# Chunks of 32 rows in place of 16, with descriptors up to 64 KB, in a streaming RMSNorm + ReLU

## Chip, cores, metric

One NeuronCore of one Trainium2 chip. The metric is the device time of one execution in microseconds (us).

## The reference

```python
# x: (16, 1024, 512) float32, gamma: (512,) float32, eps: 1e-5
def reference(x, gamma, eps):
    rms = np.sqrt(np.mean(x ** 2, axis=-1, keepdims=True) + eps)
    return np.maximum(x / rms * gamma, 0).astype(np.float32)
```

That is 16,384 rows of 2 KB: 33.55 MB in, 33.55 MB out, and little arithmetic. Each of the 128 partitions gets 128 rows.

## The kernel before

Rows come in chunks of 16 per partition into six slots of a ring in SBUF, are normalised in place and are stored from there. One queue, that of SyncE (SP), issues all the large transfers in a fixed order. ScalarE (ACT) takes the sums of squares and the square root, VectorE (DVE) the rest, in groups of 8 rows.

```python
K = 16; G = 8; nslots = 6; per = K // G        # 8 chunks, 16 groups
xv = x2.rearrange("(c p k) d -> c p k d", p=P, k=K)   # 16 rows of a partition: 32 KB in one run
loads = [(0, 0, G), (0, G, K - G)] + [(i, 0, K) for i in range(1, nchunks)]

def store(i):
    nc.sync.wait_ge(done, per * (i + 1))
    nc.sync.dma_start(out=ov[i], in_=slot_ap(i)).then_inc(sem_slot[i % nslots], 16)

# ... SyncE's order:
for m, (i, a, r) in enumerate(loads):
    if i < nslots:
        load(m)                        # seven loads fill the ring
nc.sync.wait_ge(tick3, 6)              # hold: third row of VectorE's group 6
store(0); store(1)
for s in range(2):
    nc.sync.wait_ge(sem_slot[s], 32)   # store s has landed
    load(7 + s)                        # the last two chunks
nc.sync.wait_ge(tick1, 11)             # hold: first row of group 11
for i in range(2, nchunks):
    store(i)
# ... VectorE, for each group of 8 rows:
#   reciprocal (8 columns), then 8 x scalar_tensor_tensor (row * rstd * gamma),
#   with tick1 and tick3 counted at rows 0 and 2, then tensor_scalar_max over 8 rows -> done += 1
# ... SyncE at the end: waits for all stores
```

## Time and profile before

| | before |
|---|---|
| time, median of the first 3 runs | 162.25 us (162.23 to 162.32) |
| span of the profiled run | 160.4 us |
| packets of the transfer queue, share of 16 engines | 97.6% |
| VectorE busy | 126.0 us, 79% |
| VectorE's last instruction ends | 146.5 us |
| last packet ends | 158.8 us |

How to read this: when one resource is busy for 97.6% of the span, the others matter only where they make it wait. So the useful views are those of the stretches in which it could wait: the start, the end, and every place where a store waits for VectorE or a load for a store. The lines are in the prediction.

In addition to the views I read the packets' own records in the trace (size, start, duration). The records don't name the engine; I take a chain of packets that follow each other without a break to be one of the 16 DMA engines.

### The profile page before, as it was taken

Reading aid. Unit: us, or ns where it says so; the run is one execution under the profiler, and the core shown is the slowest. Engines: PE = TensorE matmul, PEld = TensorE weight load, DVE = VectorE, ACT = ScalarE, POOL = GpSimd, SP = SyncE. Lnnn points to the kernel's source line nnn. Section 1 sums busy time; section 2 is a strip of 40 time slices with the busy share of each in tenths; the row PEclk is TensorE's granted clock in tenths of the full one; section 3 lists DMA queues with packets and bytes.
Section 4 is the critical chain, followed back from the end, with each engine's and each line's share of the span. In section 5 each row is a group of like instructions: output and inputs, shape, how many; then the busy total and the mean of one; then the engine's idle time right before and its main releaser. Section 6 shows DMA issues by size and latency. Waiting matters only on the chain. (4 is left out here: it accounts for less than half of the span.)

```text
span 160.4 us, 1008 instructions
## 1 busy us (share of the span) xinstructions
DVE 126.0 (79%) x164; ACT 86.3 (54%) x273; POOL 0.2 (0%) x4
## 2 busy tenths in 40 slices
DVE  1103989898989999999999999999999999995000
ACT  3088919889989988988910298899400000000000
POOL 0000000000000000000000000000000000000000
DMA  5999999999999999999999999999999999999993
GB/s 168 419 441 437 490 400 400 499 409 392 482 433 392 433 474 400 409 499 400 392 466 433 409 425 466 417 400 482 425 392 482 425 400 474 433 400 466 425 409 139
DMA packets 2456, 67.12 MB, mean 419 GB/s; under 512 B 276, under 2 KB 276, under 8 KB 280
## 3 DMA queue, kind: packets, MB, share of 16 engines
q1 hardware_dynamic: 2448, 67.11, 97.6%
q10 hardware_dynamic: 8, 0.01, 0.0%
HBM read 33.56 MB, written 33.55 MB: 419 GB/s over the span
## 5 line engine op out<-in xcount | busy, mean ns | idle before, releaser
L152 DVE SCALAR_TENSOR_TENSOR slots<-slots,rstd,gamma_sb 128x512 f32 x128 | 86.2, 747 | 4.8 <-DVEq L149 4.8
L128 ACT ACTIVATE junk<-slots 128x512 f32 x128 | 74.5, 582 | 22.2 <-ACTq L124 22.0
L163 DVE TENSOR_SCALAR slots<-slots x16 | 36.7, 2294 | 2.4 <-DVEq L162 0.2
L128 ACT ACTIVATION_READ_ACCUMULATOR junk<-slots x128 | 23.9, 187 | 0.0
L146 DVE RECIPROCAL rstd<-rms x16 | 3.2, 197 | 6.2 <-DVEq L142 6.2
L135 ACT ACTIVATE rms<-ss,eps_sb x16 | 4.8, 301 | 3.0 <-ACTq L134 3.0
L139 DVE LOAD_MASK_SELECT gamma_sb<-gseed x1 | 0.0, 14 | 6.0 <-DMA gseed<-in_gamma_dram 6.0
L120 ACT ACT_TABLE_LOAD x1 | 1.3, 1283 | 2.8 <-issue 2.8
L113 DVE MEMSET gseed<- 128x512 f32 x1 | 0.5, 485 | 1.1 <-SPq L93 1.1
L139 DVE STREAM_SHUFFLE gamma_sb<-gseed 128x512 f32<-128x512 f32 x1 | 0.7, 716 | 0.0
L188 POOL MEMSET const-bfloat16-1.0<- 128x1 bf16 x1 | 0.1, 102 | 0.0
L188 POOL MEMSET const-uint8-127<- 128x1 uint8 x1 | 0.1, 102 | 0.0
L188 POOL MEMSET const-float32-1.0<- 128x1 f32 x1 | 0.1, 99 | 0.0
L188 POOL MEMSET const-float32-0.0<- 128x1 f32 x1 | 0.1, 98 | 0.2 <-issue 0.2
L114 DVE MEMSET eps_sb<- 128x1 f32 x1 | 0.1, 59 | 0.0
## 6 DMA issues: line engine op xcount, KB each, us to landing
out_dram<-slots SPq DMA_DIRECT2D x8, 4096.0 KB, 20.7
slots<-in_x_dram SPq DMA_DIRECT2D x7, 4096.0 KB, 30.3
slots<-in_x_dram SPq DMA_DIRECT2D x2, 2048.0 KB, 9.6
gseed<-in_gamma_dram ACTq DMA_DIRECT2D x1, 8.0 KB
```

The lines of the kernel that those rows point to most:

```text
L113: nc.vector.memset(gseed, 0.0).then_inc(sem_z, 1)
L114: nc.vector.memset(eps_sb, eps).then_inc(sem_z, 1)
L120: nc.scalar.preload_act_table(ACTF.Sqrt)
L128: a = nc.scalar.activation(out=junk[:, j, :], in_=slots[:, bass.ds(base + j * d, d)], func=ACTF.Square, accum_out=ss[:, bass.ds(col + j, 1)])
L135: nc.scalar.activation(out=rms[:, bass.ds(col, G)], in_=ss[:, bass.ds(col, G)], func=ACTF.Sqrt, bias=eps_sb, scale=inv_d).then_inc(sq, 1)
L139: nc.vector.stream_shuffle(gamma_sb, gseed, [0] * 32)
L146: nc.vector.reciprocal(out=rstd[:, bass.ds(col, G)], in_=rms[:, bass.ds(col, G)]).then_inc(sv, 1)
L152: r = nc.vector.scalar_tensor_tensor(out=row, in0=row, scalar=rstd[:, bass.ds(col + j, 1)], in1=gamma_sb, op0=ALU.mult, op1=ALU.mult)
L163: nc.vector.tensor_scalar_max(out=blk, in0=blk, scalar1=0.0).then_inc(done, 1)
L188: nc = _bacc.Bacc("TRN2", target_bir_lowering=False, num_devices=1)
```

## The change

Fewer and larger transfers: chunks of 32 rows (64 KB in one run per partition), a ring of three chunks, first and last chunk in pieces so that the pipeline starts and ends early, and stores held back until the loads' last packets are near.

```diff
-    K = 16
-    nslots = 6
+    K = 32
+    room = 3 * K
...
-    loads = [(0, 0, G), (0, G, K - G)] + [(i, 0, K) for i in range(1, nchunks)]
+    order = [(L, 0, 0, 8), (L, 0, 8, 8), (L, 0, 16, 16), (L, 1, 0, 32), (L, 2, 0, 32),
+             (S, 0, 0, 8), (S, 0, 8, 24),
+             (L, 3, 0, 8), (L, 3, 8, 24),
+             (S, 1, 0, 32), (S, 2, 0, 32), (S, 3, 0, 16), (S, 3, 16, 16)]
+    sems = [tc.alloc_semaphore(f"t{m}") for m in range(len(order))]
...
-        nc.sync.wait_ge(tick3, 6)
-        store(0)
-        store(1)
-        for s in range(2):
-            nc.sync.wait_ge(sem_slot[s], 32)
-            load(7 + s)
-        nc.sync.wait_ge(tick1, 11)
-        for i in range(2, nchunks):
-            store(i)
+        for m, (kind, i, a, r) in enumerate(order):
+            if (kind, i, a) == (S, 0, 0):
+                nc.sync.wait_ge(tick, 6)          # second row of group 6
+            elif (kind, i, a) == (S, 1, 0):
+                nc.sync.wait_ge(done, 10)
+            elif kind == L and i == 3:
+                stored(0, a, r)
+            transfer(m)                           # a store waits for its groups in `done`
...
-                if j == 0:
-                    r.then_inc(tick1, 1)
-                if j == 2:
-                    r.then_inc(tick3, 1)
+                if j == 1:
+                    r.then_inc(tick, 1)
```

An entry (L or S, chunk, first row, rows) is a load or a store.

More of the change, by code (lines that the diff above doesn't have):

```diff
@@ L32 @@
     inv_d = 1.0 / d
-    K = 16
     G = 8
+    ngroups = rows // G
+    K = 32
     nchunks = rows // K
-    nslots = 6
-    ngroups = rows // G
-    per = K // G
+    room = 3 * K
     xv = x2.rearrange("(c p k) d -> c p k d", p=P, k=K)
@@ L51 @@
     rstd = singles.tile([P, rows], F32, name="rstd")
-    slots = singles.tile([P, nslots * K * d], F32, name="slots")
+    buf = singles.tile([P, room * d], F32, name="buf")
     junk = psum.tile([P, G, d], F32, name="junk")
-    loads = [(0, 0, G), (0, G, K - G)] + [(i, 0, K) for i in range(1, nchunks)]
-    sem_half = tc.alloc_semaphore("half")
-    sem_slot = [tc.alloc_semaphore(f"slot{s}") for s in range(nslots)]
+    L, S = 0, 1
+    order = [(L, 0, 0, 8), (L, 0, 8, 8), (L, 0, 16, 16), (L, 1, 0, 32), (L, 2, 0, 32),
[3 more added lines that the diff above has]
+    sems = [tc.alloc_semaphore(f"t{m}") for m in range(len(order))]
     sem_g = tc.alloc_semaphore("gam")
@@ L64 @@
     sq = tc.alloc_semaphore("sq")
-    tick1 = tc.alloc_semaphore("tick1")
-    tick3 = tc.alloc_semaphore("tick3")
+    tick = tc.alloc_semaphore("tick")
     done = tc.alloc_semaphore("done")
@@ L69 @@
     sv = tc.alloc_semaphore("sv")
-    def slot_ap(i):
-        s = (i % nslots) * K * d
-        return slots[:, s:s + K * d].rearrange("p (k d) -> p k d", d=d)
-    def load(m):
-        i, a, r = loads[m]
-        nc.sync.dma_start(out=slot_ap(i)[:, a:a + r, :],
-                          in_=xv[i][:, a:a + r, :]
-                          ).then_inc(sem_half if m == 0 else sem_slot[i % nslots], 16)
-    def loaded(engine, m):
-        i = loads[m][0]
-        if m == 0:
-            engine.wait_ge(sem_half, 16)
-        else:
-            engine.wait_ge(sem_slot[i % nslots], 32 * (i // nslots) + 16)
@@ L88, in store, with transfer @@
-    def store(i):
-        nc.sync.wait_ge(done, per * (i + 1))
-        nc.sync.dma_start(out=ov[i], in_=slot_ap(i)).then_inc(sem_slot[i % nslots], 16)
+    def transfer(m):
+        kind, i, a, r = order[m]
+        row = (i * K) % room + a
+        here = buf[:, row * d:(row + r) * d].rearrange("p (k d) -> p k d", d=d)
+        there = (ov if kind == S else xv)[i][:, a:a + r, :]
+        if kind == S:
+            nc.sync.wait_ge(done, (i * K + a + r) // G)
+            nc.sync.dma_start(out=there, in_=here).then_inc(sems[m], 16)
+        else:
+            nc.sync.dma_start(out=here, in_=there).then_inc(sems[m], 16)
@@ L92, with stored @@
+    def stored(i, a, r):
+        nc.sync.wait_ge(sems[order.index((S, i, a, r))], 16)
     ctx.enter_context(tc.manual_schedule(engines={mybir.EngineType.SP}))
     with tc.tile_critical():
-        for m, (i, a, r) in enumerate(loads):
-            if i < nslots:
-                load(m)
-        nc.sync.wait_ge(tick3, 6)
-        store(0)
-        store(1)
-        for s in range(2):
-            nc.sync.wait_ge(sem_slot[s], 32)
-            load(7 + s)
-        nc.sync.wait_ge(tick1, 11)
-        for i in range(2, nchunks):
-            store(i)
@@ L109 @@
-        for m, (i, a, r) in enumerate(loads):
-            loaded(nc.gpsimd, m)
-            nc.gpsimd.sem_inc(ready, r // G)
+        for m, (kind, i, a, r) in enumerate(order):
[6 more added lines that the diff above has]
+            transfer(m)
+        for m, (kind, i, a, r) in enumerate(order):
+            if kind == L:
+                nc.gpsimd.wait_ge(sems[m], 16)
+                nc.gpsimd.sem_inc(ready, r // G)
@@ L124 @@
             nc.scalar.sem_inc(ready, -1)
-            base = nc.scalar.snap((gi % (nslots * per)) * (G * d))
+            base = nc.scalar.snap((gi % (room // G)) * (G * d))
             col = nc.scalar.snap(gi * G)
@@ L128 @@
                 a = nc.scalar.activation(
-                    out=junk[:, j, :], in_=slots[:, bass.ds(base + j * d, d)],
+                    out=junk[:, j, :], in_=buf[:, bass.ds(base + j * d, d)],
                     func=ACTF.Square, accum_out=ss[:, bass.ds(col + j, 1)])
@@ L142 @@
             nc.vector.sem_inc(sq, -1)
-            base = nc.vector.snap((gi % (nslots * per)) * (G * d))
+            base = nc.vector.snap((gi % (room // G)) * (G * d))
             col = nc.vector.snap(gi * G)
-            blk = slots[:, bass.ds(base, G * d)]
+            blk = buf[:, bass.ds(base, G * d)]
             nc.vector.reciprocal(out=rstd[:, bass.ds(col, G)],
@@ L150 @@
             for j in range(G):
-                row = slots[:, bass.ds(base + j * d, d)]
+                row = buf[:, bass.ds(base + j * d, d)]
                 r = nc.vector.scalar_tensor_tensor(
@@ L165 @@
     with nc.sync.register("landed") as landed:
-        nc.sync.reg_mov(landed, 32)
-        for s in range(nchunks - nslots, nslots):
-            nc.sync.wait_ge(sem_slot[s], landed)
-        nc.sync.reg_mov(landed, 64)
-        for s in range(nchunks - nslots):
-            nc.sync.wait_ge(sem_slot[s], landed)
+        nc.sync.reg_mov(landed, 16)
+        for m, (kind, i, a, r) in enumerate(order):
+            if kind == S:
+                nc.sync.wait_ge(sems[m], landed)
 _INS = ['x', 'gamma', 'eps']
```

## The prediction

> **What bounds the kernel now.** I read the page's busy shares first, then the 40 slices, then the DMA queues, then the timeline of the queue that issues the transfers. From the page:
>
> ```profile
> span 160.4 us, 1008 instructions
> ...
> DVE 126.0 (79%) x164; ACT 86.3 (54%) x273; POOL 0.2 (0%) x4
> ...
> DVE  1103989898989999999999999999999999995000
> ACT  3088919889989988988910298899400000000000
> ...
> DMA  5999999999999999999999999999999999999993
> ...
> q1 hardware_dynamic: 2448, 67.11, 97.6%
> ```
>
> The DMA row is full from the second slice to the last but one, and the queue line puts its packets at 97.6% of sixteen engines' span: 0.976 x 160.4 = 156.5 us per DMA engine. Only 3.9 us are not packet time. VectorE (DVE) ends four slices earlier. The stretches view says the same:
>
> ```profile
> 0.00:4.00 4.00, 0.49 (x2) 1.24 (x1) 0.20 (x4) 1.00 0.55 168
> 4.00:56.00 52.00, 39.90 (x53) 40.99 (x133) 0.00 (x0) 1.00 1.00 433
> ...
> 76.00:84.00 8.00, 7.55 (x11) 4.70 (x16) 0.00 (x0) 1.00 0.93 393
> ```
>
> The last two columns are DMA share and GB/s; packets are booked where they start, so short stretches wobble. The kernel is bound by the DMA engines, and a change can win only by (a) cheaper packets, (b) fewer gaps, (c) a shorter head or tail. But one chain runs close beside them:
>
> ```profile
> 0.94 3.62 SPq L77 DMA_DIRECT2D slots<-in_x_dram  x7
> 58.35 0.82 SPq L90 DMA_DIRECT2D out_dram<-slots  x2
> 71.54 10.28 SPq L77 DMA_DIRECT2D slots<-in_x_dram  x2
> 98.23 48.62 SPq L90 DMA_DIRECT2D out_dram<-slots  x6
> ```
>
> The last store is issued near 146.5 us (98.23 + 48.62 is its end), when VectorE's last group is done (next lines). It sits right behind the seventh store.
>
> ```profile
> 14.53 0.20 DVE L146 RECIPROCAL rstd<-rms  x1 [6.24 <-DVEq L142]
> ...
> 47.51 0.20 DVE L146 RECIPROCAL rstd<-rms  x1
> ...
> 138.17 0.20 DVE L146 RECIPROCAL rstd<-rms  x1
> ...
> 144.20 2.29 DVE L163 TENSOR_SCALAR slots<-slots  x1
> ```
>
> A group of 8 rows costs VectorE (138.17 - 14.53)/15 = 8.243 us, without a stall from the first group to the last: the chain is 14.53 + 16 x 8.243, about 146.5.
>
> **What the Trainium skill says.** "DMA: Bandwidth & Descriptors", section "Why small descriptors are slow (HBM only)": a small fixed overhead per packet, which matters for descriptors of some hundred bytes. The packet records agree: the median is 0.611 us for 16 KB and 1.213 us for 32 KB, so 0.602 us per 16 KB and a fixed 0.009 us. Same page, "Where 436 GB/s comes from": the ports carry 435 GB/s; the trace shows 433 in the steady stretch, so larger descriptors have almost nothing left to win. Same page, "Latency and other measured facts": first byte after about 600 ns from this kind of queue; in this trace the first load is issued at 0.94 and the sixteen engines start their first packets between 1.95 and 2.85, so 1.0 to 1.9 us (I use these). The same section warns of HBM row pitches that are large powers of two (slow from 2 MiB, still near full at 512 KiB); here the pitch between partitions goes from 32 KB to 64 KB, well below, and no run yet shows it.
>
> **The change part by part.**
>
> *Packets.* A transfer of 128 partitions puts 8 descriptors on each engine (136 records per engine = 17 transfers x 8). Before, per engine: 15 transfers of 32 KB rows and 2 of 16 KB: 120 x 1.213 + 16 x 0.611 = 155.3 us. After: four of 64 KB (loads 1 and 2, stores 1 and 2), two of 48 KB, three of 32 KB, four of 16 KB. By the line above, 64 KB is 0.009 + 4 x 0.602 = 2.417 us and 48 KB 1.815: 32 x 2.417 + 16 x 1.815 + 24 x 1.213 + 32 x 0.611 = 155.0 us. Transfers fall from 17 to 13, each with a completion record of 0.009 us. Sum: **0.3 us saved**, 0.2%. The measured packets were 0.97 us per engine over 155.3: 0.65 in the first 8 us, 0.15 near 76 to 80 us. The first three loads do not change, so that start stays.
>
> *Head.* The same three loads come first, so the first group still starts at 14.5.
>
> *VectorE's supply.* Loads 2 and 3 become one of 32 rows. In the trace the old second of the two lands at 42.38 us; the new one at about 42.3 (8 packets of 2.417 in place of 16 of 1.213 save 0.07). From landing to VectorE's start took 14.53 - 8.38 = 6.15 us for the first group (the relay, eight squares on ScalarE (ACT), one square root). Group 5 can therefore start at 48.4, and VectorE is free at 47.5: **a new stall of 0.9 us**. Load 2 (lands near 61.7) is early, its group is due at 81. So everything on VectorE from group 5 on is 0.9 later, and its end moves from 146.5 to 147.4.
>
> *First stores behind the loads.* The signal moves to the second row of group 6: 57.15 + 2 x 0.67 = 58.5 us, against 58.35. The loads' packets run to about 60.7 on the earliest engine, so with 1.0 to 1.9 us of issue latency no gap opens, before or after.
>
> *Reloads.* Store 0 in pieces (8 and 24 rows) lets load 3's first piece be issued when 8 rows are stored, at about 66, in place of 71.5 for 16 rows. It waits in the queue behind the 24 rows anyway, so this gain is hidden. Its second piece is issued at about 81.1, with the first piece's packets running to about 85: covered.
>
> *Stores of the second half.* Store 1 waits for 10 groups: 97.0 + 0.9 = 97.9, issued about 98.0 (before 98.23). The reloads' packets end about 99.7 to 100.2, and new packets arrive 99.0 to 99.9: just covered. Store 2 needs group 12 (114.4, due at 119), the next piece group 14 (130.9, due at 138.5).
>
> *The last store.* Still 16 rows, 8 packets of 1.213 us per engine = 9.70 us. Before, the queue reached it at 148.15 to 149.2 (packets of the store ahead, taken as 0.4 us before its semaphore steps of 148.55 to 149.65) and it had been issued at 146.53: 1.6 us of slack or more. After: issued at 147.43, first packets 148.4 to 149.3; the engines are free at 147.85 to 148.9. So a **gap of up to 0.6 us** opens on each engine and eats the 0.3 us saved. The end is 148.4 to 149.3 plus 9.7 = 158.1 to 159.0, against 157.85 to 158.84 before. The slowest engine counts: between -0.3 and +0.2 us. The remaining 0.5 us to landing and 1.05 us of closing instructions stay.
>
> **The rivals.**
> 1. *Larger descriptors give real bandwidth*, as the change intends. For: the mean over the span is 419, not 433. Against: the shortfall is head and tail, about 1.95 + 1.5 us, which no packet size touches. Even with all 0.97 us of slow packets also gone: 162.25 - 0.3 - 0.97 = 161.0.
> 2. *The late end of VectorE becomes the bound* (the 0.9 us stall). It has 1.6 us of slack, of which 1.0 to 1.9 are issue latency. If latency is like the first load's worst, the end is 0.3 to 0.7 later: 162.6 to 163.0. If it is at its best, as it may be in a warm queue: 162.0.
> 3. *64 KB packets run slower than the line says* (pitch, a limit in the engine, less even progress). Nothing in this trace tests sizes above 32 KB. A 1% loss on 32 packets x 2.417 = 77 us is 0.8 us: 163.0. A loss over 2% of the kernel's time needs 3.3 us, 4% on each of these packets.
> 4. *The gap at store 1 opens*, if the reloads finish early or the signal comes late: up to 0.5 us more.
>
> **Range and chances.** The sum is -0.3 (packets, completions) + 0.0 to 0.6 (gap at the last store), so about 0 to +0.2 for the likeliest latency: 162.2 us. Rival 1 in part gives the low end, 161.6; rivals 2 or 3 the high end, 162.9. Faster by 2% means 159.0, and that lies under the floor: 155.0 of packets, 1.95 of head, 1.5 of tail and the 1.9 by which the time exceeds the span make 160.4: 1%. Slower by 2% means 165.5, which needs 64 KB rows to go wrong: 2%. The rest is within 2%.
>
> **What would show it.** Right: q1's share of the span stays near 97 to 98%; packets of 64 KB have a median of 2.41 to 2.42 us; VectorE's reciprocal of group 5 waits about 0.9 us beyond the short idle times, and its last instruction ends near 147.4; the DMA row stays full to the last slice but one. Wrong: 64 KB packets above 2.45 us; a gap at 99 to 100 us; a last store whose packets start over 1 us after the store ahead has ended; or a DMA row with dips, which would mean that I missed a wait between a store and the load that takes its place.

## More of the kernel before

A hold, in this document, is a wait that keeps back a store whose rows are already done.

By **extra time** I mean a packet's duration less the median of its size, summed over a stretch and divided by 16: what an average engine lost there. In the experiments, packets that are over by 0.05 us or less are left out of it.

## The result

| | before | changed |
|---|---|---|
| time, median of 4 runs | 162.28 us (162.23 to 162.32) | 162.21 us (161.84 to 162.33) |
| ratio | | 0.9992, 95% interval 0.9975 to 1.0009 |
| span of the profiled run | 160.4 us | 160.1 us |
| packet time per engine, from the packet records | 156.30 us | 156.11 us |

A ratio is the mean time of one kernel's runs over that of the other's runs of the same rounds, so it is not quite the ratio of the medians quoted beside it. Executions over 1.5% slower than the fastest of the same kernel are left out of the means. The profiled run of the changed kernel was its fastest (161.84); the other three took 162.13 to 162.33.

From the page of the changed kernel, the same lines as before: span, busy shares, the DMA row of the 40 slices, the transfer queue with packets, MB and share.

```profile
span 160.1 us, 1001 instructions
...
DVE 126.1 (79%) x164; ACT 86.3 (54%) x273; POOL 0.2 (0%) x4
...
DMA  5999999969969979999999999799799999899993
...
q1 hardware_dynamic: 1872, 67.11, 97.6%
```

The packets fall from 2448 to 1872 and the share stays at 97.6%. The 6s and 7s in the row are not idle time: a packet is booked in the slice in which it starts, and a 64 KB packet takes more than half of a 4 us slice. In the packet records the breaks of over 0.04 us sum to only 0.13 us per engine. So the "DMA row with dips" that the prediction named as a sign of being wrong is here, but without a wait behind it.

The queue of SyncE (start, extent, what was issued, how many):

```profile
0.94 2.61 SPq L79 DMA_DIRECT2D buf<-in_x_dram  x5
58.37 0.82 SPq L77 DMA_DIRECT2D out_dram<-buf  x2
66.39 15.30 SPq L79 DMA_DIRECT2D buf<-in_x_dram  x2
97.75 49.78 SPq L77 DMA_DIRECT2D out_dram<-buf  x4
```

Store 0 goes out at 58.37, as before (58.35). The reload's first piece goes out at 66.39 in place of 71.54 and gains nothing, since its packets come behind 24 rows of store. VectorE at groups 4 to 5, and its last instruction:

```profile
44.99 2.29 DVE L150 TENSOR_SCALAR buf<-buf  x1
48.18 0.20 DVE L135 RECIPROCAL rstd<-rms  x1 [0.89 <-DVEq L131]
...
144.88 2.29 DVE L150 TENSOR_SCALAR buf<-buf  x1
```

The bracket on the second line is new: VectorE stood idle for 0.89 us ahead of group 5, because load 1 lands in one piece of 32 rows. Its end moves from 146.5 to 147.2.

### The profile page after: what moved, and what is told of

It is laid out like the page before. It is cut to its first block, busy times and chain, and to the rows that moved or that the text cites. A ratio compares the mean times of both kernels' runs of the same rounds, so it can differ in the third digit from the quotient of the medians.

```text
span 160.1 us, 1001 instructions
## 1 busy us (share of the span) xinstructions
DVE 126.1 (79%) x164; ACT 86.3 (54%) x273; POOL 0.2 (0%) x4
## 3 DMA queue, kind: packets, MB, share of 16 engines
q1 hardware_dynamic: 1872, 67.11, 97.6%
## 5 line engine op out<-in xcount | busy, mean ns | idle before, releaser
L141 DVE SCALAR_TENSOR_TENSOR buf<-buf,rstd,gamma_sb 128x512 f32 x128 | 86.2, 747 | 4.8 <-DVEq L138 4.8
L117 ACT ACTIVATE junk<-buf 128x512 f32 x128 | 74.5, 582 | 26.2 <-ACTq L113 26.2
L150 DVE TENSOR_SCALAR buf<-buf x16 | 36.7, 2294 | 2.4 <-DVEq L149 0.2
L117 ACT ACTIVATION_READ_ACCUMULATOR junk<-buf x128 | 23.9, 187 | 0.0
```

Source lines behind the costliest of these rows:

```text
L117: a = nc.scalar.activation(out=junk[:, j, :], in_=buf[:, bass.ds(base + j * d, d)], func=ACTF.Square, accum_out=ss[:, bass.ds(col + j, 1)])
L141: r = nc.vector.scalar_tensor_tensor(out=row, in0=row, scalar=rstd[:, bass.ds(col + j, 1)], in1=gamma_sb, op0=ALU.mult, op1=ALU.mult)
L150: nc.vector.tensor_scalar_max(out=blk, in0=blk, scalar1=0.0).then_inc(done, 1)
```

## The experiments

The prediction held, so the questions are where the small gain went, how near VectorE is to the path, and why this order of the queue works at all. The first theory, A, was the prediction's: only packet time counts, and the 0.9 us stall eats the gain at the last store. Its first rival, B: the stall lies in slack.

The closing waits of the kernel (on a register's value, right ahead of a branch) were not available for the experiments, so most of them wait on constants instead. The control measures that. All but the last experiment have the control's closing waits, and their edits are shown against it.

### c0_control: the closing waits on constants

```diff
-    with nc.sync.register("landed") as landed:
-        nc.sync.reg_mov(landed, 16)
-        for m, (kind, i, a, r) in enumerate(order):
-            if kind == S:
-                nc.sync.wait_ge(sems[m], landed)
+        for m, (kind, i, a, r) in enumerate(order):
+            if kind == S:
+                nc.sync.wait_ge(sems[m], 16)
```

> The changed kernel with its closing waits taken on constants instead of a register; nothing else. It is the base for the other runs. Both theories: 162.2 to 162.6 us (the closing instructions may cost up to 0.3 us more), packets of 64 KB 2.418 us, the wait of VectorE's fifth reciprocal 0.9 us, last store issued near 147.2 to 147.5.

Measured: ratio to before 1.0008 (0.9994 to 1.0021), 162.21 to 162.87 us. From its last packet to the end of the span pass 1.94 us, against 1.57 in the changed kernel: 0.4 us of closing instructions. The rest is like the changed kernel. Its issues of store 0, of the reload and of the later stores, which the next runs are held against:

```profile
58.50 0.82 SPq L77 DMA_DIRECT2D out_dram<-buf  x2
66.56 15.29 SPq L79 DMA_DIRECT2D buf<-in_x_dram  x2
97.89 49.78 SPq L77 DMA_DIRECT2D out_dram<-buf  x4
```

### c1_load1_halves, c2_last_store_8, c3_both: is it the stall?

```diff
 c1:  -(L, 1, 0, 32),               +(L, 1, 0, 16), (L, 1, 16, 16),
 c2:  -(S, 3, 16, 16)]              +(S, 3, 16, 8), (S, 3, 24, 8)]
 c3:  both
```

> Load 1 in two halves of 16 rows. Theory A (the 0.9 us stall eats the gain at the last store): the stall goes, VectorE's last instruction ends 0.9 us earlier, the last store is issued near 146.3 to 146.5 and no engine waits between the last two stores; time 0.05 to 0.3 us below the control. Theory B (the stall lies in slack, and the runs differ by their start alone): the stall goes too, but the time stays within 0.1 us of the control.

> The last 16 rows stored in two pieces of 8. The stall of 0.9 us stays. Theory A: the last store now has the 4.9 us of the piece before it as slack, so no engine waits for VectorE at the end; 0.05 to 0.3 us below the control. Theory B: within 0.1 us of the control, or 0.02 slower by one more completion record and 8 packets of 16 KB per engine at 0.009 us more per 32 KB (0.08 us).

> Both edits. Theory A: no more than either alone, 0.05 to 0.3 us below the control, about 162.0, with a narrower spread than the control. Theory B: within 0.1 us of the control. Neither expects more than 0.5 us, since the packets alone take 156.1 us of each engine.

Measured: c1 1.0050 (1.0027 to 1.0072), c2 1.0011 (0.9991 to 1.0031), c3 1.0041 (1.0027 to 1.0055). Neither theory had this. In c1 the stall did go (group 5 starts at 47.3 us without a bracket, VectorE ends 1.0 us earlier than in the control), and yet c1 is **slower**. c2 is the same as the control, so slack for the last store gains nothing that these runs can see. The start of group 5 in the control, then in c1:

```profile
48.32 0.20 DVE L135 RECIPROCAL rstd<-rms  x1 [0.87 <-DVEq L131]
```

```profile
47.32 0.19 DVE L135 RECIPROCAL rstd<-rms  x1
```

Something that came with the missing stall did harm. The queue of c1 shows the difference:

```profile
57.49 0.82 SPq L77 DMA_DIRECT2D out_dram<-buf  x2
67.36 15.08 SPq L79 DMA_DIRECT2D buf<-in_x_dram  x2
```

Store 0 is released by a row of VectorE's group 6, which is now 1.0 us earlier: 57.49 in place of 58.50. But its first piece lands 0.8 us *later*, which the second line shows, since the reload waits for just that: 67.36 in place of 66.56. The packet records say where the time went. Each engine's last packet of load 2, 64 KB, started between 58.2 and 58.7 us and took 0.35 to 1.1 us longer than the median of 2.418. All sixteen did, and none ahead of them. In the control two of them did, by 0.06 and 0.26. Load 2 was complete at 62.41 in place of 61.55. In c3 store 0 went out at 57.51, and all sixteen last packets ran longer again, by the same 0.80 us per engine as in c1.

This gave theory E: a load packet that starts while a store is already waiting behind it in its engine's queue runs longer. (The table below shows where this wording fails.)

### d4_no_hold: the stores queued as early as possible

```diff
-            if (kind, i, a) == (S, 0, 0):
-                nc.sync.wait_ge(tick, 6)
-            elif (kind, i, a) == (S, 1, 0):
-                nc.sync.wait_ge(done, 10)
-            elif kind == L and i == 3:
+            if kind == L and i == 3:
                 stored(0, a, r)
```

> The two holds are taken out: store 0 is issued when its rows are done (its first piece near 22.5 us, its second near 47.2) and store 1 after 8 groups (near 81.4), both queued far behind loads. Theory A (one queue per engine serves in the order of issue, so the time of issue doesn't matter while it is early enough): within 0.2 us of the control. Theory D (a store queued among loads mixes reads and writes and slows the loads): loads 1 and 2 land later by 1 us or more, and the time is 0.5 to 2 us above.

Measured: 1.0069 (1.0057 to 1.0081), 1.0 us above the control by the two ratios. Store 0's two pieces went out at 22.7 and 47.4:

```profile
22.69 25.07 SPq L77 DMA_DIRECT2D out_dram<-buf  x2
67.70 14.97 SPq L79 DMA_DIRECT2D buf<-in_x_dram  x2
82.72 64.91 SPq L77 DMA_DIRECT2D out_dram<-buf  x4
```

Theory A failed here and theory D was half right. Load 1, with a store queued behind it all the time, landed at 42.14 us (control 42.20), so loads in general are not slowed. Only the last packet of load 2 on each engine was, by 0.75 to 1.5 us: extra time of 1.22 us per engine in the stretch of 54 to 66 us, against 0.02. In the view of stretches (start:end, length, then busy time by engine, clock, DMA share, GB/s; packets booked at their start), first the control:

```profile
60.00:64.00 4.00, 3.85 (x5) 4.00 (x13) 0.00 (x0) 1.00 0.88 377
```

then the run without holds:

```profile
60.00:64.00 4.00, 3.85 (x5) 4.00 (x13) 0.00 (x0) 1.00 0.58 250
```

The same compute, and a third fewer bytes begun, since the engines are still at their last load packets. So the first hold, which looks like a wait that could only cost, is worth about 1 us. The second hold is out here too, and at its turn the loss is small: store 1 went out at 82.72 in place of 97.89, and the reload's last packets, which ended at 100.5 to 101.3, were longer by at most 0.15 us (0.04 us per engine; the control has 0.03). In e2 below, this turn costs 0.15, against 0.00 in the kernel before.

### e1_halves_hold_later: c1 with the hold put right

```diff
 (c1, and)
-                if j == 1:
+                if j == 3:
                     r.then_inc(tick, 1)
```

> Load 1 in halves as in c1, which was slower (ratio 1.0050) although VectorE's stall went, and the signal that releases store 0 two rows later (fourth row of group 6), so the store is issued near 58.8 us in place of 57.5. Theory E (a load packet that starts on an engine while a store is already queued behind it runs up to 1.5 us longer; c1's store came before the last packets had started): the extra time of the last 64 KB packets falls from 0.8 us per engine to under 0.15, and the ratio to before falls from 1.005 to 0.999 to 1.002. Theory F (the two more transfers or the order of completions in c1 cost the time): ratio stays near 1.005.

Measured: 1.0024 (1.0006 to 1.0042), 162.30 to 163.26 us. The packet part of theory E came true in full:

```profile
58.91 0.82 SPq L77 DMA_DIRECT2D out_dram<-buf  x2
66.47 15.32 SPq L79 DMA_DIRECT2D buf<-in_x_dram  x2
```

Store 0 went out 1.4 us later than in c1 and its first piece landed 0.9 us earlier. No load packet at that turn ran longer: the extra time of 54 to 66 us is 0.004 us per engine against 0.80 in c1. The one more transfer and semaphore of c1 (the expectation says two) were not the cause of that. The ratio, though, fell only from 1.0050 to 1.0024, short of the range expected. Its interval overlaps the control's and c1's, so the clock settles neither that e1 equals the control nor that it is faster than c1. Theory E beat theory F in the packets and not in the time.

### e2_before_no_hold: does it go with the size of the packet?

```diff
 (the kernel before, with closing waits on constants)
-        nc.sync.wait_ge(tick3, 6)
         store(0)
         store(1)
 ...
-        nc.sync.wait_ge(tick1, 11)
```

> The kernel before with its two holds taken out and its closing waits on constants (worth about +0.3 us by the first control): store 0 issued near 31, store 1 near 47.6, behind loads of 32 KB rows. Theory E1 (the last load packets are lengthened whatever their size): 0.8 to 1.3 us per engine of extra time in the packets of 57 to 62 us, as with 64 KB rows without hold (1.23), time 1.0 to 1.5 us above before. Theory E2 (the extra time goes with the size of the packet): about half, 0.4 to 0.7 us per engine, 0.7 to 1.0 above before. Theory G (it is a matter of 64 KB rows alone): under 0.1 us per engine, 0.2 to 0.4 above.

Measured: 1.0042 (1.0029 to 1.0055), 0.7 us above before, at the low edge of theory E2. Part of that is the closing waits: no run has the kernel before with these alone, so what its missing holds cost in time is not shown. The stores went out at 31 and 47.5 us:

```profile
30.98 16.83 SPq L90 DMA_DIRECT2D out_dram<-slots  x2
71.96 10.33 SPq L77 DMA_DIRECT2D slots<-in_x_dram  x2
```

The reload is 0.42 us later than before (71.54). The last 32 KB packet of each engine took 0.2 to 0.9 us more, 0.61 us per engine. That fits theory E2: half the packet, half the loss (0.61 at 32 KB, 1.22 at 64 KB), from this one pair of sizes. Both kernels lose packet time without their holds, and with the larger descriptor twice as much.

These turns in one table, from the packet records (without d3, whose 2 KB packets overlap); the stretch of 54 to 66 us holds the turn from loads to stores, that of 74 to 86 the turn back.

| run | store 0 issued, us | last load packets, KB | extra, 54 to 66 | extra, 74 to 86 | load of the full ring landed, us |
|---|---|---|---|---|---|
| before | 58.35 | 32 | 0.01 | 0.15 | 61.79 |
| changed | 58.37 | 64 | 0.05 | 0.31 | 61.50 |
| c0_control | 58.50 | 64 | 0.02 | 0.29 | 61.55 |
| c1_load1_halves | 57.49 | 64 | 0.80 | 0.02 | 62.41 |
| c2_last_store_8 | 58.42 | 64 | 0.06 | 0.25 | 61.71 |
| c3_both | 57.51 | 64 | 0.80 | 0.03 | 62.34 |
| d1_load1_late | 63.43 | 48 | 0.00 | 0.77 | 61.66 |
| d2_rows_16k | 59.49 | 16 | 0.00 | 0.20 | 62.76 |
| d4_no_hold | 22.69, 47.42 | 64 | 1.22 | 0.00 | 62.80 |
| e1_halves_hold_later | 58.91 | 64 | 0.00 | 0.13 | 61.66 |
| e2_before_no_hold | 30.98, 47.46 | 32 | 0.61 | 0.01 | 62.22 |
| e3_reload_hold | 58.53 | 64 | 0.03 | 0.21 | 61.57 |
| f1_retuned | 59.18 | 64 | 0.00 | 0.29 | 61.56 |

Against the control, d4's sums (+1.20 at the first turn, -0.29 at the second) make 0.92 us, and the ratios say 1.0. For c1, +0.78 and -0.27 make 0.51, and the ratios say 0.7; for c3 0.52 and 0.5. For e1 the sums make -0.17 and the ratios say +0.3, so there they don't explain the clock. The sums are averages over engines, and the slowest engine sets the time: the profiled executions of c1 and of the control were equally long (161.0 us each), because the control's slowest engine ended 0.9 us behind the average and c1's 0.5 us. That c1 is slower rests on its six runs.

Theory E as worded doesn't fit every row. In the kernel before, store 0 was issued at 58.35 and the last load packets started at 59.58 to 60.14, which is 1.2 to 1.8 us later. From an issue to the first packet on idle engines pass 0.84 to 0.99 us (d1, below), so the store should have been waiting when they started; still they ran longer by at most 0.08 us. In d2 it is the same (issue 59.49, last load packets from 60.56 to 61.69). So the start of the last load packet is not the edge. What the runs bracket is the issue: at 57.5 us or before it was dear, at 58.35 or later it cost at most 0.06 us per engine. Counted back from the end that a last load packet would have had, the issue lay at least 3.16 us ahead in the dear runs and at most 3.01 us in the others. That edge was found afterwards, and no run tests it.

### d1_load1_late: how near is VectorE?

```diff
-             (L, 1, 0, 32), (L, 2, 0, 32),
+             (L, 2, 0, 8), (L, 1, 0, 32), (L, 2, 8, 24),
```

The edit also sorts the relay's waits on GpSimd, so that the groups are still handed on in the order of their rows.

> The first 8 rows of load 2 are fetched ahead of load 1, so load 1 lands 4.85 us later (near 46.9) and VectorE's stall at group 5 grows from 0.9 to about 5.8 us; bytes and packets nearly as before. Theory A (VectorE's chain runs under 1 us behind the DMA engines): the first store is issued near 63.2 while the loads' packets end near 60.6, so a gap of about 3 us opens there and about 1.5 us more by the last store; 4.3 to 5.0 us above the control, about 166.8. Theory B (VectorE is far off the path, the transfers hide it): under 1 us above.

Measured: 1.0265 (1.0250 to 1.0280), 166.55 to 166.77 us, 4.2 us above the control by the ratios. Theory A's figure was just missed and theory B is out. Store 0 came too late:

```profile
63.43 0.82 SPq L77 DMA_DIRECT2D out_dram<-buf  x2
69.76 15.85 SPq L79 DMA_DIRECT2D buf<-in_x_dram  x2
```

and in its stretches not one packet starts between 60 and 64 us:

```profile
60.00:64.00 4.00, 3.70 (x6) 4.00 (x14) 0.00 (x0) 1.00 0.00 0
```

By the packet records the engines stood still for 3.1 to 3.7 us here and for 0.5 to 1.0 us ahead of the last store, 4.2 us per engine in all. Store 0 went out 4.93 us later than in the control, the last store 4.92, and 4.2 of this reach the end: the changed schedule absorbs about 0.7 us. Not all of this is slack of VectorE, for the control's slowest engine ended 0.9 us behind the average and d1's only 0.1. This run also measures by itself what the prediction had to guess: from the issue at 63.43 to the first packets on sixteen idle engines pass 0.84 to 0.99 us, and 0.83 to 0.98 at 152.26.

### d2_rows_16k, d3_rows_2k: what is a large descriptor worth?

Another assignment of rows to partitions cuts each descriptor to 8 rows or to 1 row. Order, sizes and waits of the transfers stay.

```diff
 d2:
-    xv = x2.rearrange("(c p k) d -> c p k d", p=P, k=K)
+    xv = x2.rearrange("(c h p k) d -> c p h (k d)", h=K // G, p=P, k=G)
 d3:
+    xv = x2.rearrange("(c k p) d -> c p k d", p=P, k=K)
 (the same for ov; in d2 the slices that use them follow)
```

> Same transfers in the same order, but every descriptor cut to 8 rows (16 KB) by another assignment of rows to partitions: 256 packets per engine of 0.611 us = 156.4 us against 155.0. Theory A (only the fixed 0.009 us per packet counts): 1.2 to 1.5 us above the control, near 163.7. Theory C (large descriptors carry bandwidth of their own, through longer bursts): more than 2.5 us above.

> As the run before, with one row (2 KB) per descriptor: 2048 packets per engine. Theory A: by the fit 0.084 us each, 172 us per engine, so 17 us above the control, near 179. Theory C: the cost per packet grows as packets shrink, well over 185.

Measured: d2 1.0093 (1.0080 to 1.0107), 1.4 us above the control, as theory A had it (1.2 to 1.5). d3 1.1008 (1.0990 to 1.1026), 16.2 us above the control; theory A had 17. From d3's page:

```profile
DMA packets 32984, 67.12 MB, mean 379 GB/s; under 512 B 212, under 2 KB 212, under 8 KB 32984
```

The median of its 2 KB packets is 0.085 us; the line through 16 and 32 KB gave 0.084. With the 64 KB packets at 2.418 (predicted 2.417) one straight line, 0.602 us per 16 KB plus 0.009 us per packet, holds from 2 to 64 KB. In these runs size counts 0.009 us for each packet saved and nothing else: theory C is out.

### e3_reload_hold: is there such a hold for the turn from stores to loads?

```diff
             elif kind == L and i == 3:
                 stored(0, a, r)
+                if a == 0:
+                    nc.sync.wait_ge(tick7, 8)   # seventh row of group 8
```

> The control with one more hold: load 3's first piece, which waits in the queue behind store 0 from 66.5 us on, is issued only at the seventh row of group 8, near 78.2 us, while the store's last packets of 48 KB (started 78.0 to 78.5) run. Theory E taken over to a load behind a store: the 0.29 us per engine of extra time in the packets of 78 to 81 us falls under 0.1, and the time is 0.1 to 0.3 us below the control's ratio of 1.0008. If writes before reads are not concerned: the extra time stays at 0.2 to 0.3 us and the time stays the same.

Measured: 1.0027 (0.9981 to 1.0074), inconclusive. Of six runs three took 162.10 to 162.27 us and three 164.22 to 164.56 (two of these count as slow runs). The profiled run is one of the short ones. In it the store's last 48 KB packets no longer ran longer (one did, by 0.06), but the first 16 KB packets of the reload did, and the extra time of 74 to 86 us is 0.21 against 0.29. The loss moved rather than went. What makes the long runs is open: none of them was profiled.

### f1_retuned: the changed kernel with what was learnt

```diff
 (the changed kernel)
-             ... (S, 3, 16, 16)]
+             ... (S, 3, 16, 8), (S, 3, 24, 8)]
...
-                if j == 1:
+                if j == 2:
                     r.then_inc(tick, 1)
...
                 nc.sync.wait_ge(sems[m], landed)
+        nc.sync.sem_inc(fin, 1)
```

> The changed kernel with its own closing waits (a register that holds 16, followed by one more semaphore instruction), store 0 released one row later (near 59.1 us, after every engine has started its last load packet and about 1.5 us before the first one is through), and the last 16 rows stored in two pieces of 8. If the hold and the last store are all that the changed kernel left open: extra time of the packets of 54 to 62 us under 0.02 us per engine, no engine waiting before the last store, 161.8 to 162.2 us, ratio to before 0.996 to 0.999. If the spread of its runs comes from elsewhere: ratio 0.999 to 1.001, and a spread as wide as the changed kernel's.

Measured: 0.9997 (0.9980 to 1.0013), 161.87 to 162.82 us. The turn is clean (0.00 us extra), no engine waits more than 0.05 us ahead of the last stores, and the time is still that of the kernel before and of the changed one. So the hold and the last store are not what is left, and the spread of the runs has another cause. No version beat the two kernels beyond the noise.

## Why the prediction was right

The time alone tests little of the prediction. Its terms are 0.3 to 0.6 us and partly cancel, and the changed kernel's runs spread over 0.5 us, so the terms have to be checked one by one.

- **The bound.** Right: 97.6% of the engines' span is packets before and after. (A slip without weight: VectorE ends three slices before the DMA row, not four.)
- **Packets.** Right: medians of 2.418 and 1.815 us for 64 and 48 KB, as worked out. The saving was 0.2 us per engine instead of 0.3, since the turn back from stores to loads cost 0.31 us of extra time in place of 0.15. d2 and d3 confirm the fixed 0.009 us.
- **VectorE's stall.** Right: 0.89 us (predicted 0.9), end at 147.2 (147.4; this run started 0.3 us earlier).
- **The last store.** Right in kind, too large in size. The gap was to be up to 0.6 us on each engine; in the profiled run three engines waited 0.1 to 0.3 us, in the control five, by 0.13 to 0.37. The mis-sized term is the issue latency of 1.0 to 1.9 us, taken from the first load: in the running kernel it is 0.83 to 0.99 us (d1). c2 took the gap away and gained nothing measurable.
- **First stores behind the loads.** Here the step was too simple. I asked only if a store comes too late, and wrote that no gap opens, which was so. The runs showed a second edge: a store that is issued 0.9 us earlier (c1, c3) lengthens the load packet ahead of it. The change lies between the edges: store 0 at 58.37 us, 0.9 us after c1's, and the earliest engine free at 60.46. None of my rivals had this; it did not move the result because the change's author had placed the hold well, which for the prediction was luck.
- **Rivals.** Rivals 1 and 3 are out: 64 KB packets lie on the line. Rival 2 is real in kind, as d1 shows, but the change stays inside its slack except for the waits of three engines above. Rival 4, a gap at the second half's first store, did not occur: its packets follow the reload's.

**Open.** Why an early store lengthens the packet ahead of it, and why less at the later turn (0.04 us in d4, 0.15 in e2), is not shown; no run here looks inside an engine. Also open: why the turn back from stores to loads was free (0.00 to 0.03 us) in just those runs in which the first turn was dear, and dear (0.77) in d1, and what spreads the changed kernel's runs over 0.5 us. The packets' ends point at the slowest engines: in the changed kernel the last engine is 0.37 us behind the median when the loads end near 61 us and 0.6 at the end; in the control it goes from 0.2 to 1.0, in the kernel before from 0.3 to 0.8. But long and short runs were not profiled side by side.

## What to carry to other kernels

When the DMA engines are busy from the first microsecond to the last, larger descriptors buy only the fixed cost of the packets saved, here 0.009 us each, so count the packets before rewriting a schedule. At the first turn of this kernel, a store behind loads in one queue has a window: not as early as 57.5 us, when it lengthened the last load packets, and not later than the issue latency of about 1 us before the engines come free. Its early edge was bracketed and not explained, so don't carry its place over; and anything that shifts the compute, even for the better, shifts the signal that opens it. Measure the hold again after each such edit.

## What the Trainium skill lacked or had wrong

- "DMA: Bandwidth & Descriptors", section "Rules for kernel authors", advises to issue a DMA early and wait on it late. It lacks the exception seen here: a store queued long ahead behind loads on the same engines lengthened each engine's last load packet at the first turn, by 0.61 us at 32 KB and 1.22 us at 64 KB on average, and the time by about 1.0 us (d4).
- The same page, "Latency and other measured facts", gives about 600 ns to the first byte for this kind of queue. It doesn't say from which moment. Counted from the end of the issuing instruction, which takes 0.34 us, d1 shows 0.50 to 0.65 us to the first packet on idle engines, which agrees; from its start it is 0.83 to 0.99 us, and for the kernel's first load 1.0 to 1.9 us.
- No page has a measured fixed cost of a packet of some KB: here 0.009 us each from 2 KB to 64 KB, beside 0.602 us per 16 KB.
